# A planned one-core kernel: later products, a half-height low part of Q, fewer row transfers, one more score buffer

## The chip, the cores and the metric

The kernel runs on one core of a Trainium2 chip. The metric is the device time of one execution in microseconds (us). The core has TensorE (PE in the profile, its weight loads PEld), VectorE (DVE), ScalarE (ACT), GpSimd (POOL) and the sync engine SP, which here issues every DMA. Each engine works through its own instructions in order.

## What is computed

One layer of a streaming encoder, for a prompt of 2048 frames and for 32 new frames with a cache, with 1024 features. Two branches read the same normalised input `h`: attention over a band of nine chunks of 64 frames, and a gated delta rule. They are gated, merged and projected, and a layer norm ends the layer.

```python
qa, ka, va, za, qkv_b, zb, a_b, b_b, gate_a, gate_b = split_projection(x @ w_in)
oa = chunk_band_attention(qa, ka, va, rel_bias)          # 8 heads of 64
ya = (oa.reshape(bsz, t, A_WIDTH) * jax.nn.silu(za)) @ w_branch_a
...
yb = (ob * jax.nn.silu(zb)) @ w_branch_b
mix = jax.nn.sigmoid(gate_a) * ya + jax.nn.sigmoid(gate_b) * yb
y = layer_norm(ALPHA * x + mix @ w_out, ln_g, ln_b)
```

Outputs are `y` for both inputs, the newest 512 rows of K and V (`nk_p`, `nv_p`), the 32 new rows (`nk_s`, `nv_s`), and the states of the other branch.

## The kernel before

**Stages.** The prompt is worked in two halves of 1024 frames. Each half has the delta rule (`phase_b`) and then attention (`phase_a`). Both run beside the projections `x @ w_in`, which are cut into jobs of 128 output columns: the matmuls `pj<-hi,whi`, `pj<-hi,wlo` and `pj<-lo,whi`, since values are split into a high and a low fp16 part. The projections are PE's bulk work, and whatever else PE has to do lies between them. At the end `merge` multiplies the branches by their output weights (`a<-ghi,whi` and others) and finishes the rows.

**What sets the order.** The program is written out when it is built. Generators (one for each job, score, product and so on) run in a small event planner, the class `Flow` (line 163 on), that keeps a clock for every engine and for the DMA queue. An instruction is laid down when its generator's turn comes by these clocks, and so each engine's order is fixed. `Engine.price` gives the planned time of an instruction, and `Flow.transfer` that of a DMA. A DMA transpose is issued by `turn`. The planner gives it SP's usual 0.5 us for the issue, then its size over a rate, and then `MARGIN` = 1.6 us. What `turn` returns is the planned landing, and the product is laid down no earlier than that. On the chip only semaphores count: an instruction laid too early waits, and all that is behind it on its engine waits with it. The profile gives almost every instruction one line, L269, since `Engine` makes them all; `dma` is L292 and `turn` is L303. So the tile names tell the operations apart.

**Attention** (`phase_a`). Heads are worked in four pairs. A pair has jobs for V, K, Q and the gate z:

- `job_v`: V into `vf`, then split and turned by DMA into `vt`. In the second half V's newest 512 rows go out through `rows_out`.
- `job_k`: K split into `kst`, 128 rows for each head: high part in the head's own 64 rows, low part in the other 64.
- `job_q`: Q split into a high part `qd`, which stands in both row halves, and a low part `ql`. In `ql` each head has 128 rows, of which the 64 that aren't its own are zeros, written once for each of two buffers. Each block of Q needs four transfers for `qd` and two for `ql`, one for each head.

For each of the 8 tiles of 128 frames, and each of the 2 heads, there is a `score` and a `product`. `score` multiplies `qd` and `ql` with `kst` in one or two pieces of at most 512 keys into a PSUM bank (`a<-kst,qd`, `a<-kst,ql`). VectorE adds the bias and takes the maximum, into a score buffer `sb`. ScalarE makes the exponential, a split into two fp16 parts goes into `pu`, and `turn` lays them out transposed in `pt`. `product` multiplies `pt` with `vt` (`c<-vt,pt`, 3 matmuls for each 128 keys), then frees the buffer `pt`. Once both heads are through, `store` scales the result, turns it on PE (`b<-ident,ob`), multiplies it by the gate `ga`, which comes by DMA from `za`, and writes `g`.

Buffers: 3 each of `sb`, `pu` and `pt` in the second half, 4 in the first.

**Row outputs.** `rows_out` turns 128 columns at a time on PE into a bank of their own, copies them with ScalarE into one of two buffers `ro`, and sends them out, one transfer for each 128 rows. V's 512 rows take four transfers, K's last two blocks (272 and 240 rows) three and two, and the 32 new rows one.

**The new frames** (`sample`) have scores of their own. There the 32 rows' Q (`qs`) and the cached K are read in the head's own 64 rows only: `a<-part,qs` and `a<-ks,qs`, fp32 matmuls of 64 rows by 32 columns.

Of the kernel before, what the change touches and what calls it, by code (L numbers as in the profile page):

```python
# [11 lines left out]
F32 = mybir.dt.float32  # L12
# [45 lines left out]
    ORDER += [(_p, 0), (_p, 1), (_p, 2), (_p - 1, 3)] + [None] * FILL[_p]  # L58
ORDER += [(NP - 1, 3)]
MARGIN = 1.6  # L60
LEAD = 5.0
ZERO = 1.2
BLOCKS = [
# [214 lines left out]
def trunk(ctx: ExitStack, tc: tile.TileContext, x_p, x_s, cache_k, cache_v, st_conv, st_gdn,  # L278
# [11 lines left out]
    def dma(dst, src, eng=nc.sync):  # L290

        eng.dma_start(dst, src)  # L292
        size = 2 if dst.dtype == F16 else 4
        n = size
        for k in dst.shape:
            n *= k

        n = max(n, n // (size * dst.shape[-1]) * 768)
        return flow.transfer("SP" if eng is nc.sync else "S", n)

    def turn(dst, src):

        nc.sync.dma_start_transpose(dst, src)  # L303
        n = 2 * P
        for k in dst.shape[1:]:
            n *= k
        return flow.transfer("SP", n * 1.5)

    def gate(n):
        return Gate(flow, n)  # L310
# [21 lines left out]
    def pt(tag):  # L332

        return bank_pool[tag].tile([P, 512], F32, tag=tag, bufs=banks[tag], name=tag)
# [1157 lines left out]
    def phase_a(half):  # L1492
# [5 lines left out]
        KW = base + HALF  # L1498
        done = mark()
        vf_slot, vt_slots, kst_slots, q_slots = gate(1), gate(2), gate(2), gate(2)  # L1500
        ro_slots, bias_slots, vs_slot, sample_slot = gate(2), [gate(2), gate(1)], gate(2), gate(1)
        last_block = len(BLOCKS[half]) - 1
        NPART = 4
        parts = [ap.tile([P, 2, 512], F16, name=f"part{i}") for i in range(NPART)]
# [15 lines left out]

        low_q = []
        for i in range(2):
            t = ap.tile([P, 2, HALF], F16, name=f"ql{i}")
            for h in range(2):
                G.memset(t[HS[1 - h], h], 0.0)
            low_q.append(t)
        pairs = []
        for p in range(NP):  # L1530
            k = Pair()
# [21 lines left out]

        def rows_out(src, n, dst, p):

            for t in range(0, n, P):
                m = min(P, n - t)
                yield bank["b"]
                ps = pt("b")
                PE.transpose(ps[:m, 0:P], src[:, t:t + m], ident[:])  # L1560
                yield ro_slots
                ro = ap.tile([P, P], F32, tag="ro", bufs=2, name="ro")
                S.copy(out=ro[:m], in_=ps[:m, 0:P])
                bank["b"].give()
                yield
                yield dma(dst[t:t + m, p * P:(p + 1) * P], ro[:m])
                ro_slots.give()

        def job_v(k):
            p = k.p  # L1570
# [8 lines left out]
            def rest():  # L1579
# [32 lines left out]
                if last:  # L1612
                    yield bank["b"]
                    ps = pt("b")
                    PE.transpose(ps[:DEC, 0:P], vf[:, KW:KW + DEC], ident[:])
                    k.v_s = ap.tile([DEC, P], F32, tag="v_s", bufs=2, name="v_s")
                    S.copy(out=k.v_s[:], in_=ps[:DEC, 0:P])
                    bank["b"].give()
                    k.v_s_done.done()
                    yield  # L1620
                    yield from rows_out(vf[:, KW - BAND:KW], BAND, nv_p, p)
                    yield from rows_out(vf[:, KW:KW + DEC], DEC, nv_s, p)
                vf_slot.give()

            def evac(bi, c0, n, gcol, ps):
# [59 lines left out]
        def job_q(k):  # L1685
# [3 lines left out]
            def begin():  # L1689
                nonlocal qd, ql  # L1690

                u = k.unit = ap.tile([P, 4], F32, tag="unit", bufs=2, name=f"unit{p}")
                V.tensor_tensor(out=u[:, 0:1], in0=w_inv[:, p:p + 1], in1=w_inv[:, 4 + p:5 + p], op=ALU.mult)
                V.tensor_scalar(out=u[:, 0:1], in0=u[:, 0:1], scalar1=HD ** -0.5 / SMALL ** 2, scalar2=None, op0=ALU.mult)
                V.tensor_scalar(out=u[:, 1:2], in0=u[:, 0:1], scalar1=-1.0, scalar2=None, op0=ALU.mult)
                V.reciprocal(out=u[:, 2:3], in_=u[:, 0:1])
                V.tensor_tensor(out=u[:, 3:4], in0=w_inv[:, p:p + 1], in1=u[:, 2:3], op=ALU.mult)
                V.tensor_scalar(out=u[:, 3:4], in0=u[:, 3:4], scalar1=HD ** -0.5, scalar2=None, op0=ALU.mult)
                k.unit_known.done()
                k.qd = qd = ap.tile([P, 2, HALF], F16, tag="qd", bufs=2, name=f"qd{p}")  # L1700
                k.ql = ql = low_q[p % 2]
                k.q_s = ap.tile([P, DEC], F32, tag="q_s", bufs=2, name=f"qs{p}") if last else None

            def evac(bi, c0, n, gcol, ps):
# [13 lines left out]
                for h in range(2):  # L1718
                    for o in range(2):
                        dma(qd[HS[o], h, cs], hi[HS[h], 0:m])  # L1720
                    t = dma(ql[HS[h], h, cs], lo[HS[h], 0:m])
                yield t
                part_slots.back(place)
                if bi == last_block:
# [38 lines left out]
            pass  # L1763

        og_slots = places(4)
        NSB, NPU, NPT = (3, 3, 3) if last else (4, 4, 4)
        sbs = [ap.tile([P, KEYS], F32, name=f"sb{i}") for i in range(NSB)]
        pus = [ap.tile([P, 2 * KEYS], F16, name=f"pu{i}") for i in range(NPU)]
        pts = [ap.tile([P, 10, P], F16, name=f"pt{i}") for i in range(NPT)]
# [34 lines left out]
        def score(h, k, t, w, place, before, turn_):  # L1804
# [8 lines left out]
            for i, (s0, sn) in enumerate(pieces):  # L1813
# [2 lines left out]
                PE.matmul(ps[:, 0:sn], qd[:, h, t * P:(t + 1) * P], kst[:, h, kc + s0:kc + s0 + sn],  # L1816
                          start=True, stop=False)
                yield
                PE.matmul(ps[:, 0:sn], ql[:, h, t * P:(t + 1) * P], kst[:, h, kc + s0:kc + s0 + sn],
                          start=False, stop=True)  # L1820
                yield
                V.tensor_tensor_reduce(out=sb[:, s0:s0 + sn], in0=ps[:, 0:sn],
# [69 lines left out]
        def store(k, t, gt, w):  # L1892
# [4 lines left out]
            for z, (c0, n, _) in zip(k.z, BLOCKS[half]):  # L1897
                if c0 < (t + 1) * P:
                    yield z
            at = dma(ga[:], za_dram[k.p][:, gt * P:(gt + 1) * P])  # L1900
            yield
            ob = obs[place]
            for h in range(2):
# [520 lines left out]
```

## Time and profile before

| | us |
|---|---|
| median of 3 runs (2076.62 to 2083.29) | 2080.12 |
| the profiled execution, its own time | 2078.09 |
| its span in the profile | 2076.3 |
| PE busy | 1930.5 |
| DVE busy | 1400.7 |
| ACT busy | 972.5 |
| POOL busy | 796.0 |
| first half's attention, roughly | 550 to 800 |
| second half's attention, roughly | 1350 to 1700 |

How to read it: the profile shows one execution. "Busy" is the time in which an engine had an instruction of the program in work. A matmul row such as `c<-vt,pt 128*128 128x64 f16` names the output and inputs, the rows and columns of the weights (128 by 128), and the size and type of the moving operand. Matmuls overlap, so a row's duration (0.38 us for 512 columns) is longer than the spacing from one start to the next (0.22 us), and it is the spacing that adds up. In brackets stands how long the engine idled before the instruction, and what ended it. `SPq` rows are DMA issues: their time is SP's, not the transfer's. PEclk and the figure behind the busy times of a stretch are the clock that TensorE was granted, as a share of the full one.

### The profile page before, as it was taken

The page shows a single profiled execution, that of the slowest core. Times are in us where ns is not written, and L with a number is a line of the kernel's source. Part 1 is how long each engine was busy: PE and PEld are TensorE (multiplying, and loading weights), DVE is VectorE, ACT ScalarE, POOL GpSimd, SP SyncE. Part 2 cuts the span into 40 slices and gives each one's busy share as a digit, 9 for nine tenths or more (in the row PEclk, how much of TensorE's full clock was granted, in tenths as well). Part 3 has the DMA queues.
Part 4 walks back from the last instruction along what each step waited for, and adds up shares of the span by engine and source line. Part 5 has one row for each costly group of instructions (what it writes and reads, how often), then busy time and mean ns, then how long its engine had stood idle before and what let it go on. Part 6 is the DMA issues. An engine that isn't in the chain of part 4 may idle for free. (4 is left out here: it accounts for less than half of the span.)

```text
span 2076.3 us, 41078 instructions
## 1 busy us (share of the span) xinstructions
PE 1930.5 (93%) x14517; PEld 1353.4 (65%) x14517; DVE 1400.7 (67%) x4498; ACT 972.5 (47%) x2002; POOL 796.0 (38%) x1139
## 2 busy tenths in 40 slices
PE   8999999999989899999999999998888879999997
PEld 5455666665444446576776777665555568999996
DVE  7789889852556658589889884254545468665665
ACT  6655545444655667665445434354646552111110
POOL 6444334333334334443333423132323245543452
PEclk9999999999999999999999999999999989999999
DMA  4124332332587775223232333466776785433331
GB/s 138 65 87 112 87 85 75 102 90 98 140 201 158 163 171 135 69 81 87 74 84 67 94 98 90 117 142 146 158 167 148 186 217 193 132 102 122 103 124 46
DMA packets 380055, 246.85 MB, mean 119 GB/s; under 512 B 251202, under 2 KB 328366, under 8 KB 379848
## 3 DMA queue, kind: packets, MB, share of 16 engines
q1 hardware_dynamic: 379848, 244.22, 44.4%
q8 instruction: 114, 1.87, 0.4%
q14 instruction: 93, 0.76, 0.1%
HBM read 140.11 MB, written 54.72 MB: 94 GB/s over the span
## 5 line engine op out<-in xcount | busy, mean ns | idle before, releaser
L269 PE MATMUL pj<-hi,whi 128*128 128x512 f16 (+2 forms) x1992 | 651.3, 342 | 10.6 <-DVE zb L269 3.1
L269 PE MATMUL pj<-hi,wlo 128*128 128x512 f16 (+2 forms) x1952 | 643.6, 342 | 0.6 <-POOL wlo L269 0.5
L269 PEld LDWEIGHTS <-whi 128*128 128x128 f16 x3984 | 414.7, 106 | 226.0 <-issue 11.9
L269 PE MATMUL pj<-lo,whi 128*128 128x512 f16 (+2 forms) x1992 | 460.3, 343 | 0.0
L269 POOL TENSOR_TENSOR wlo<-wraw,whi 128x256 f16<-128x256 f32 x384 | 266.7, 718 | 497.4 <-ACT whi L269 369.5
L269 PEld LDWEIGHTS <-wlo 128*128 128x128 f16 x1952 | 207.1, 106 | 122.8 <-issue 16.6
L269 ACT CAST mh<-sg 128x256 fp32r<-128x256 f32 x64 | 25.8, 407 | 278.2 <-DVE sg L269 259.1
L269 ACT ACTIVATE wraw<-wraw,w_scale 128x1024 f32<-128x1024 f32 (+1 forms) x98 | 111.4, 1136 | 84.2 <-DVE w_scale L269 82.7
L269 ACT ACTIVATE sb<-sb,mx,unit 128x640 f32<-128x640 f32 (+4 forms) x128 | 108.5, 848 | 68.9 <-DVE mx L269 59.1
L269 PE MATMUL a<-ghi,whi 128*128 128x256 f32 (+1 forms) x512 | 134.4, 292 | 6.7 <-DVE sg L269 6.1
L269 POOL TENSOR_TENSOR pu<-sb,pu 128x640 f16<-128x640 f32 (+2 forms) x64 | 81.7, 1277 | 146.1 <-ACT pu L269 92.9
L269 ACT CAST whi<-wraw 128x512 f16<-128x512 f32 (+1 forms) x196 | 119.2, 611 | 33.3 <-PE pj L269 30.5
L269 PE MATMUL c<-vt,pt 128*128 128x64 f16 x1680 | 74.6, 198 | 64.5 <-DMA pt<-pu 61.4
L269 PE MATMUL a<-ghi,wlo 128*128 128x256 f32 (+1 forms) x512 | 132.0, 288 | 1.1 <-POOL wlo L269 1.0
L269 PEld LDWEIGHTS <-pt 128*128 128x128 f16 x1680 | 65.8, 101 | 98.8 <-DMA pt<-pu 87.1
L269 DVE TENSOR_TENSOR sys_u<-sys_u,sys_t 128x60 f32<-128x60 f32 (+24 forms) x527 | 124.6, 242 | 5.7
L269 DVE CUSTOM_DVE_ANT_0 sb<-a,bias 128x320 f32<-128x320 f32 (+5 forms) x136 | 66.5, 498 | 77.0 <-PE a L269 71.5
L269 DVE SCALAR_TENSOR_TENSOR acc<-raw,cwT,acc 128x512 f32<-128x512 f32 x144 | 112.8, 783 | 8.1 <-ACT acc L269 6.8
L269 DVE TENSOR_TENSOR sys_t<-sys_u,sys_p 128x60 f32<-128x60 f32 (+21 forms) x459 | 110.0, 243 | 5.5
L269 PEld LDWEIGHTS a<-ghi,whi 128*128 128x128 f32 x512 | 99.5, 194 | 8.3 <-DVE sg L269 6.7
L269 PEld LDWEIGHTS a<-ghi,wlo 128*128 128x128 f32 x512 | 98.9, 193 | 1.9 <-POOL wlo L269 1.2
L269 POOL TENSOR_TENSOR w_scale<-w_scale,mhalf 128x1 f32<-128x1 f32 x49 | 31.7, 648 | 168.1 <-DVE w_scale L269 120.0
(345 smaller groups left out, 4013.5 us busy)
## 6 DMA issues: line engine op xcount, KB each, us to landing
wraw<-in_w_in SPq DMA_DIRECT2D x192, 256.0 KB
sg<-sig SPq DMA_DIRECT2D x112, 128.0 KB
sig<-sig SPq DMA_DIRECT2D x44, 256.0 KB
sys_p<-sol_p SPq DMA_DIRECT2D x68, 128.0 KB
x<-in_x_p SPq DMA_DIRECT2D x16, 512.0 KB
xt<-in_x_p SPq DMA_DIRECT2D x16, 512.0 KB
out_y_p<-xt SPq DMA_DIRECT2D x16, 512.0 KB
glo<-g SPq DMA_DIRECT2D x14, 512.0 KB
```

Of the source, the lines that this page charges most:

```text
L269: r = f(*a, **k)
```

## The change

- `turn`: the planner's SP clock goes on by 0.8 us more for each transpose, and the planned landing by `SLACK` = 2.5 us. The planned landing of the gate `ga` in `store` goes back by the same. These change only the order that is laid down.
- `ql` has one 128-row tile for both heads, without zeros, in two buffers. A block's transfer is one instead of two. The score's second matmul reads the head's own 64 rows of `ql` and of `kst`, where K's high part stands.
- `rows_out` turns up to 512 columns into one bank, copies whole tiles at once into one buffer `ro` of 512 columns, and sends the full tiles in one transfer and the rest in another. V's 32 new rows are sent from the copy that `sample` reads, without another turn on PE.
- The second half's score buffers `sb` are 4 instead of 3.

```diff
+SLACK = 2.5
...
     def turn(dst, src):
...
-        return flow.transfer("SP", n * 1.5)
+        flow.busy["SP"] = max(flow.busy.get("SP", 0.0), flow.cur.clock + 0.2) + 0.8
+        return flow.transfer("SP", n * 1.5) + SLACK
...
-        ro_slots, bias_slots, vs_slot, sample_slot = gate(2), [gate(2), gate(1)], gate(2), gate(1)
+        ro_slots, bias_slots, vs_slot, sample_slot = gate(1), [gate(2), gate(1)], gate(2), gate(1)
...
-        low_q = []
-        for i in range(2):
-            t = ap.tile([P, 2, HALF], F16, name=f"ql{i}")
-            for h in range(2):
-                G.memset(t[HS[1 - h], h], 0.0)
-            low_q.append(t)
...
         def rows_out(src, n, dst, p):
 
+            full = n // P
+            yield bank["b"]
+            ps = pt("b")
             for t in range(0, n, P):
                 m = min(P, n - t)
-                yield bank["b"]
-                ps = pt("b")
-                PE.transpose(ps[:m, 0:P], src[:, t:t + m], ident[:])
-                yield ro_slots
-                ro = ap.tile([P, P], F32, tag="ro", bufs=2, name="ro")
-                S.copy(out=ro[:m], in_=ps[:m, 0:P])
-                bank["b"].give()
-                yield
-                yield dma(dst[t:t + m, p * P:(p + 1) * P], ro[:m])
-                ro_slots.give()
+                PE.transpose(ps[:m, t:t + P], src[:, t:t + m], ident[:])
+            yield ro_slots
+            ro = ap.tile([P, 512], F32, tag="ro", bufs=1, name="ro")
+            if full:
+                S.copy(out=ro[:, 0:full * P], in_=ps[:, 0:full * P])
+            m = n - full * P
+            if m:
+                S.copy(out=ro[:m, full * P:(full + 1) * P], in_=ps[:m, full * P:(full + 1) * P])
+            bank["b"].give()
+            yield
+            cs = slice(p * P, (p + 1) * P)
+            at = 0.0
+            if full:
+                at = dma(dst[0:full * P, cs].rearrange("(t q) d -> q t d", q=P),
+                         ro[:, 0:full * P].rearrange("q (t d) -> q t d", d=P))
+            if m:
+                at = dma(dst[full * P:n, cs], ro[:m, full * P:(full + 1) * P])
+            yield at
+            ro_slots.give()
...
-                    yield from rows_out(vf[:, KW:KW + DEC], DEC, nv_s, p)
+                    yield dma(nv_s[:, p * P:(p + 1) * P], k.v_s[:])
...
-                k.ql = ql = low_q[p % 2]
+                k.ql = ql = ap.tile([P, HALF], F16, tag="ql", bufs=2, name=f"ql{p}")
...
                     for o in range(2):
                         dma(qd[HS[o], h, cs], hi[HS[h], 0:m])
-                    t = dma(ql[HS[h], h, cs], lo[HS[h], 0:m])
+                t = dma(ql[:, cs], lo[:, 0:m])
...
-        NSB, NPU, NPT = (3, 3, 3) if last else (4, 4, 4)
+        NSB, NPU, NPT = (4, 3, 3) if last else (4, 4, 4)
...
-                PE.matmul(ps[:, 0:sn], ql[:, h, t * P:(t + 1) * P], kst[:, h, kc + s0:kc + s0 + sn],
+                PE.matmul(ps[:, 0:sn], ql[HS[h], t * P:(t + 1) * P], kst[HS[h], h, kc + s0:kc + s0 + sn],
                           start=False, stop=True)
...
-            at = dma(ga[:], za_dram[k.p][:, gt * P:(gt + 1) * P])
+            at = dma(ga[:], za_dram[k.p][:, gt * P:(gt + 1) * P]) + SLACK
```

## The prediction

> **What bounds the kernel now.** I read the page first, then busy time by stretch, then who TensorE (PE) waited for, then the timelines of SP and PE around the longest waits. The page's sums and slices:
>
> ```profile
> PE 1930.5 (93%) x14517; PEld 1353.4 (65%) x14517; DVE 1400.7 (67%) x4498; ACT 972.5 (47%) x2002; POOL 796.0 (38%) x1139
> PE   8999999999989899999999999998888879999997
> PEclk9999999999999999999999999999999989999999
> ```
>
> PE is busy 93% of the span, far ahead of the others, so a microsecond of PE work or of PE idling anywhere counts whole. The dips lie where attention runs: slices 11 to 14 (first half) and 27 to 32 (second half), the only stages that the change touches. Busy time in those two stretches (columns: stretch; length, PE, PEld, DVE, ACT, POOL busy; granted clock, DMA share, GB/s):
>
> ```profile
> 550.00:850.00 300.00, 265.91 (x2058) 153.96 (x2057) 189.16 (x653) 187.62 (x374) 114.59 (x146) 0.97 0.68 160
> 1350.00:1700.00 350.00, 297.62 (x2634) 198.15 (x2632) 184.76 (x653) 194.13 (x407) 99.03 (x101) 0.93 0.70 160
> ```
>
> PE idles 34.1 us in the first and 52.4 us in the second, 86.5 of the 145.8 us (2076.3 - 1930.5) that it idles in all. Who ended that idling, over the whole span:
>
> ```profile
> PE c L269 <- DMA pt<-pu: 61.4, 42, 3.8
> PE b L269 <- DVE ga L269: 7.9, 7, 2.3
> ```
>
> The first row is the products `c<-vt,pt`: 42 of the 128 blocks of them stood in PE's queue before the transposed probabilities `pt` had landed. One such wait, on SP (which issues all DMAs in order) and on PE:
>
> ```profile
> 1519.81 0.59 SPq L292 DMA_DIRECT2D ql<-part  x1
> 1520.51 0.52 SPq L292 DMA_DIRECT2D bias<-ext_dram  x1
> 1521.13 1.11 SPq L292 DMA_DIRECT2D qd<-part  x2
> 1522.33 0.55 SPq L292 DMA_DIRECT2D ql<-part  x1
> 1522.93 1.24 SPq L292 DMA_DIRECT2D qd<-part  x2
> 1524.21 0.60 SPq L292 DMA_DIRECT2D ql<-part  x1
> 1524.92 1.34 SPq L303 DMA_TRANSPOSE pt<-pu  x1
> ```
>
> ```profile
> 1523.89 0.63 PE L269 MATMUL pj<-lo,whi 128*128 128x272 f16 x4
> 1528.34 0.61 PE L269 MATMUL c<-vt,pt 128*128 128x64 f16 x15 [3.83 <-DMA pt<-pu]
> ```
>
> SP issues without a break for 5 us, the transpose comes last, and the product starts 3.42 us after that issue began (1528.34 - 1524.92). PE's order had put it 3.83 us too early. The program's planner gave a transpose 0.5 us of SP's time; the trace says 1.34.
>
> Such a stop also costs clock. The stretch before the stop, the stop, and what follows:
>
> ```profile
> 1520.00:1524.40 4.40, 4.40 (x31) 2.84 (x29) 0.67 (x2) 0.69 (x1) 0.00 (x0) 1.00 0.53 137
> 1524.40:1528.40 4.00, 0.17 (x3) 0.06 (x3) 0.94 (x4) 0.00 (x0) 0.00 (x0) 1.00 0.58 124
> 1528.40:1536.50 8.10, 8.10 (x74) 5.75 (x75) 3.60 (x16) 2.86 (x6) 0.73 (x2) 0.79 0.55 132
> ```
>
> The granted clock falls from 1.00 to 0.79 for the 8.1 us after it: about 1.7 us more (0.21 x 8.1).
>
> **The change, part by part.** The sum is made against the profiled execution's own 2078.09 us (span 2076.3 and 1.8 around it), 0.1% under the median 2080.12.
>
> *Products later.* Planned landing moves back by 2.5 us, and the planner's SP clock by 0.8 us for each transpose. PE's order at the start of the first half's attention, before (`pt` names the transposed tile, `qd` and `ql` Q's high and low part, `pj` the projection that fills the gaps):
>
> ```order
> L269 LDWEIGHTS pt_5997
> L269 MATMUL c<-vt_6085,pt_5997 128x64
> L269 LDWEIGHTS whi
> L269 MATMUL pj<-hi_162,whi 128x512
> L269 LDWEIGHTS wlo
> L269 MATMUL pj<-hi_162,wlo 128x512
> L269 LDWEIGHTS qd_6264
> L269 MATMUL a<-kst_6168,qd_6264 128x320
> ```
>
> The same product in PE's order of the changed kernel:
>
> ```order
> L270 LDWEIGHTS qd_6258
> L270 MATMUL a<-kst_6162,qd_6258 128x320
> L270 LDWEIGHTS wlo
> L270 MATMUL pj<-hi_162,wlo 128x512
> L270 LDWEIGHTS pt_5991
> L270 MATMUL c<-vt_6079,pt_5991 128x64
> L270 LDWEIGHTS ql_6259
> L270 MATMUL a<-kst_6162,ql_6259 128x320
> ```
>
> The product stood ahead of the first 320-column score; now it stands behind the second. I counted PE work between each score's last matmul and its product through both orders, at the trace's spacing of back-to-back matmuls (0.12 us for 272 columns, below, and in proportion). The mean grows from 15.1 to 18.9 us in the first half and from 12.6 to 19.6 in the second, against a longest wait of 3.8. Work fills it: the order holds the same projections. If each wait shrinks by what its own product gained, about 19 of the 64.5 us before the products stay. They stay where the distance did not grow, as at the end of the last pair:
>
> ```profile
> 1691.85 0.60 PE L269 MATMUL c<-vt,pt 128*128 128x64 f16 x15 [1.91 <-DVE ob L269]
> 1694.37 0.82 PE L269 MATMUL c<-vt,pt 128*128 128x64 f16 x12 [1.78 <-DMA pt<-pu]
> ```
>
> SP is also relieved (below), so I take 15 us left of 61.4: **-46** (5 left: -56; 35 left, if transposes come later by as much: -26).
>
> *Clock.* Of the lost clock in the two stretches ((1 - 0.97) x 300 + (1 - 0.93) x 350 = 33 us of full clock), I put about five stops like the one above, at 1.7 us, to waits that go: **-8** (0 to -17).
>
> *Q's low part without zeros.* `ql` was a 128-row operand with 64 zero rows; now its matmul reads 64 rows. Rows of before for `ql` as read and written:
>
> ```profile
> L269 PE MATMUL a<-kst,ql x224: 217/299/490, 544.5 to 1686.4; 128*128 128x320 f16 x96, 128*128 128x384 f16 x7, 128*128 128x512 f16 x5, 128*128 128x128 f16 x4
> L292 SPq DMA_DIRECT2D ql<-part x40: 525/594/1521, 535.8 to 1621.6; - x40
> L269 POOL MEMSET ql<- x8: 945/947/993, 496.7 to 1291.5; 64x1024 f16 x8
> ```
>
> Before never reads a half-height fp16 operand with 128 columns, but it has 64-row matmuls among 128-row ones: the new frames' scores (`64*32` is 64 rows by 32 columns):
>
> ```profile
> 1375.36 0.28 PE L269 MATMUL pj<-hi,whi 128*128 128x272 f16 x1
> 1375.57 0.61 PE L269 MATMUL a<-part,qs 64*32 64x512 f32 x1
> 1376.03 0.59 PE L269 MATMUL a<-part,qs 64*32 64x512 f32 x1
> 1376.55 0.29 PE L269 MATMUL pj<-hi,wlo 128*128 128x272 f16 x1
> 1376.67 0.28 PE L269 MATMUL pj<-hi,whi 128*128 128x272 f16 x1
> 1376.79 0.28 PE L269 MATMUL pj<-hi,wlo 128*128 128x272 f16 x1
> 1377.14 0.63 PE L269 MATMUL pj<-lo,whi 128*128 128x272 f16 x4
> 1377.69 0.24 PE L269 MATMUL a<-ks,qs 64*32 64x32 f32 x2
> 1377.87 0.41 PE L269 MATMUL pj<-lo,whi 128*128 128x272 f16 x2
> ```
>
> Between 128-row matmuls of 272 columns the spacing is 0.12 us (1376.67 to 1376.79). Into 64 rows it is 0.21 (1375.36 to 1375.57): 0.09 more. Within 64 rows it is 0.46 (1375.57 to 1376.03), and out of them 0.52 (1376.03 to 1376.55): 0.06 more, and the next spacing may take another 0.01. So a visit to the 64-row form costs about 0.17 us, with the array draining twice. In the changed order the 224 `ql` matmuls stand in 208 separate runs, 198 of them alone (the last row of the fence above shows one between a product and a projection). 208 x 0.17 = **+36** on PE, nothing to hide it. Bounds: 0.14 and 0.21 give +29 and +44; nothing at all is a rival. The Trainium skill, "TensorEngine Tiling (Array Packing)", Key Properties, says that changing the tiling mode drains TensorE, while changing the tile within a mode does not. It gives no price; by that rule alone this part is a loss, and the spacings above agree.
>
> *Fewer transfers on SP.* 20 of the 40 `ql` issues go (20 x 0.59 = 12 us). So do 12 of 16 for the V rows and 4 of 20 for the K rows:
>
> ```profile
> L292 SPq DMA_DIRECT2D out_nk_p<-ro x20: 355/416/812, 1342.7 to 1638.9; - x20
> L292 SPq DMA_DIRECT2D out_nv_p<-ro x16: 338/382/655, 1340.8 to 1650.3; - x16
> ```
>
> That is 12 x 0.38 + 4 x 0.42 = 6 us more. SP's order around the transpose of the quoted wait, before (its row is the last):
>
> ```order
> L292 DMA qd_18632<-part_16103 64x512 x2
> L292 DMA ql_16105<-part_16103 64x512
> L292 DMA bias_18728<-ext_dram_99 128x640
> L292 DMA qd_18632<-part_16102 64x272 x2
> L292 DMA ql_16105<-part_16102 64x272
> L303 DMA_TRANSPOSE pt_16117<-pu_16114 128x10x128
> ```
>
> And in the changed kernel, up to the transpose of the same product:
>
> ```order
> L293 DMA ql_18538<-part_16091 128x272
> L304 DMA_TRANSPOSE pt_16104<-pu_16101 128x10x128
> L293 DMA qd_18537<-part_16092 64x240 x4
> L293 DMA ql_18538<-part_16092 128x240
> L293 DMA out_nv_s<-v_s 32x128
> L293 DMA bias_18718<-ext_dram_100 128x640
> L293 DMA ga_16107<-za_89 128x128
> L293 DMA out_nk_p<-ro 128x2x128
> L293 DMA out_nk_p<-ro 16x128
> L304 DMA_TRANSPOSE pt_16102<-pu_16099 128x10x128
> ```
>
> Each block of Q brings one `ql` transfer instead of two, and K's rows of a block go out in two. The 18 us are off the path by themselves: they are part of why 15 and not 19 us of waits stay.
>
> *The rest.* The planner's 2.5 us on `ga` put its multiplication later on VectorE; half of the 7.9 us of `PE b <- DVE ga` may go: **-4** (0 to -8). Larger row copies, eight memsets fewer on POOL, four small transposes fewer on PE, and a fourth score buffer have slack: ACT and POOL are under 63% and 39% busy in both stretches. If the longer copy of V's rows were on the path, it would cost 0.58 instead of a first piece's 0.26 us in each of four pairs, 1.3 us:
>
> ```profile
> L269 ACT COPY ro<-b 128x128 f32<-128x128 f32 (+3 forms) x39 | 9.8, 259 | 47.0 <-PE b L269 22.9 <-DMA out_nk_p<-ro 15.9 <-PE a L269 5.3
> L269 ACT COPY part<-b 128x512 f32<-128x512 f32 x4 | 2.3, 580 | 1.0 <-PE b L269 1.0
> ```
>
> The single row buffer makes the next rows wait for a landing, on ScalarE; behind it stand exponentials, whose late end reaches PE only through `pt`, in the term above.
>
> Sum: -46 - 8 + 36 - 4 = -22, so 2078.1 becomes 2056, and on the median's scale **2058 us**. Its own range, with the ends of the terms taken together in part: 2035 to 2077.
>
> **The rivals.**
>
> 1. *The waits come back, slower.* SP issues in order and was solid for 5 us ahead of the quoted transpose. If transposes are late because SP and the chain before it cannot go faster, PE merely reaches each product as far ahead again. With 45 us of waits left, no clock won back, and the 36 us of switches, it is 2078 - 16 + 36 = 2098, 2100 on the median's scale. Even is at 26 us left without any other gain, at 38 with the clock and `ga` terms. Against it: the order gives 7 us more distance in the second half where waits were at most 3.8, and SP has fewer rows. For it: places like this one, where the order now holds the product 5.8 us nearer its score and the wait was already 3.33:
>
> ```profile
> 645.55 0.66 PE L269 MATMUL c<-vt,pt 128*128 128x64 f16 x9 [3.33 <-DMA pt<-pu]
> ```
>
> 2. *Half-height matmuls cost nothing.* The extra spacing may belong to fp32 operands or to 32 columns, and an fp16 operand of 64 rows by 128 columns might pass like any other: -46 - 8 - 4 = -58, 2020, or 2022 on the median's scale. The spacings speak against it, but with other types and widths. The Trainium skill, "TensorE: Matmul & The Clock Gate" (Why this matters for your kernels), says that a small-K matmul takes the time of a full one, which would be this case; the measured spacing around it decides.
>
> 3. *They cancel.* 30 us or so of waits left and 40 of switches: -31 - 4 + 40 is +5 at most, and around zero with a little clock: 2074 to 2086.
>
> **How the numbers follow.** The forecast has 0.60, rival 1 0.17, rival 2 0.09, rival 3 0.14. Faster by over 0.3% (6.2 us, about what a measurement of this kernel can tell from no change) takes the forecast and rival 2, with an edge of the forecast on the other side: 0.68. Within 0.3%: 0.15; slower: 0.17. The range 2032 to 2090 reaches past the forecast's own range on both sides and leaves out rival 2 and the worse part of rival 1.
>
> **What would show it right or wrong.** Right: `PE c <- DMA pt<-pu` at 5 to 35 us; `a<-kst,ql` shown as `64*128`, with about 0.09 us more into it and 0.06 out of it; a granted clock over 0.95 in the second stretch. Wrong if that wait stays above 40 us (rival 1), if spacings around `ql` do not grow (rival 2), or if a new row of over 15 us stands among PE's waits, such as scores waiting for VectorE.

## The result and the profile after

The changed kernel takes 2074.04 us (median of 19 runs, 2070.44 to 2078.22), the one before 2079.59 us in the same session (median of 19, 2076.41 to 2085.61). The ratio is 0.9974 [0.9965, 0.9982]: 5.5 us faster, inside the 0.3% that the forecast took for no change, and to which it gave a chance of 0.15. The forecast was 2058 us, 22 us faster. The time is in the range, and three quarters of the gain are missing.

The profiled execution of the changed kernel took 2077.25 us (span 2075.5). The page's sums, and the clock by slices:

```profile
PE 1962.4 (95%) x14513; PEld 1340.9 (65%) x14513; DVE 1409.3 (68%) x4498; ACT 969.8 (47%) x1982; POOL 786.6 (38%) x1131
PEclk9999999999998999999999999999989979999999
```

PE works 31.9 us longer than before (1962.4 against 1930.5) and idles 32.7 us less (2075.5 - 1962.4 = 113.1 against 145.8). The two nearly cancel. Busy time in the two stretches of attention:

```profile
550.00:850.00 300.00, 282.24 (x2072) 149.80 (x2072) 196.21 (x656) 190.53 (x375) 114.46 (x147) 0.97 0.67 160
1350.00:1700.00 350.00, 314.70 (x2621) 191.44 (x2620) 186.07 (x651) 190.89 (x386) 97.07 (x99) 0.92 0.72 161
```

The whole growth of PE's busy time lies here (16.3 and 17.1 us). The granted clock did not rise: 0.97 and 0.92, against 0.97 and 0.93. Who ended PE's idle time, the longest rows of the list over the whole span:

```profile
PE c L270 <- DVE ob L270: 15.4, 11, 2.9
PE pj L270 <- ACT kr L270: 7.3, 4, 2.5
PE c L270 <- DMA pt<-pu: 6.1, 6, 3.1
PE a L270 <- DVE sg L270: 5.8, 3, 3.8
PE pj L270 <- ACT vf L270: 5.0, 2, 3.3
```

The products' wait for their transposed probabilities fell from 61.4 to 6.1 us, by more than forecast (15 left). But a product now waits for `ob`: VectorE has not yet scaled the last result out of the `c` bank. This was 2.8 us before. Projections wait more too. Both are seen in the groups:

```profile
L270 PE MATMUL pj<-hi,whi 128*128 128x512 f16 (+2 forms) x1992 | 650.5, 342 | 25.5 <-ACT kr L270 7.3 <-ACT vf L270 5.0 <-DVE mx L270 5.0
L270 PE MATMUL c<-vt,pt 128*128 128x64 f16 x1680 | 73.7, 198 | 23.5 <-DVE ob L270 15.4 <-DMA pt<-pu 6.1 <-DMA ga<-za 1.9
```

The group of products idles 23.5 us instead of 64.5, the group of projections 25.5 instead of 10.6. So 41 us went in the one and 15 came back in the other. One of the new waits, on PE, near the end of the second half:

```profile
1667.60 0.30 PE L270 MATMUL a<-kst,qd 128*128 128x320 f16 x1
1667.83 0.31 PE L270 MATMUL a<-kst,ql 64*128 64x320 f16 x1
1668.07 0.31 PE L270 MATMUL a<-kst,qd 128*128 128x320 f16 x1
1671.23 0.81 PE L270 MATMUL c<-vt,pt 128*128 128x64 f16 x15 [2.86 <-DVE ob L270]
```

And VectorE at that time:

```profile
1669.24 0.82 DVE L270 TENSOR_TENSOR pu<-sb,pu 128x640 f16<-128x640 f32 x1 [1.75 <-ACT pu L270]
1669.98 0.35 DVE L270 SCALAR_TENSOR_TENSOR ga<-b,gsc,ga 128x128 f32<-128x128 f32 x1
1670.24 0.16 DVE L270 RECIPROCAL rs<-rs 128x2 f32<-128x2 f32 x1
1670.32 0.47 DVE L270 CUSTOM_DVE_ANT_0 sb<-a,bias 128x320 f32<-128x320 f32 x1
...
1670.71 0.47 DVE L270 TENSOR_SCALAR ob<-c,rs 128x64 f32<-128x64 f32 x2
```

VectorE works through these in order. It sits behind the low part of the probabilities (`pu`), which itself waited 1.75 us for ScalarE, then does a gate, a reciprocal and a score, and only at 1670.71 reads `c`. The product starts 0.5 us later. A wait for a transfer has become a wait for VectorE, which had waited for ScalarE.

The PE rows above also show the price of a half-height matmul. From the start of `qd` to that of the 64-row `ql` are 0.23 us, from `ql` to the next matmul 0.24. The same at full height, in the kernel before:

```profile
1675.54 0.30 PE L269 MATMUL a<-kst,qd 128*128 128x320 f16 x1
1675.67 0.30 PE L269 MATMUL a<-kst,ql 128*128 128x320 f16 x1
1675.81 0.27 PE L269 MATMUL b<-ident,ob 128*128 128x128 f32 x1
```

They are 0.13 and 0.14. Over both whole traces, for 320 columns at full clock and without idling, the median is 0.136 us either way before, and 0.232 into and 0.239 out of the 64-row form after. So a visit costs about 0.10 us in and 0.10 out, 0.20 where the forecast had 0.17, and 208 visits some 42 us where it had 36. The loads of `ql`'s weights at these places, in the changed kernel and in the kernel before, differ too:

```profile
1667.83 0.09 PEld L270 LDWEIGHTS <-ql 64*128 64x128 f16 x1 [0.16 <-issue]
```

```profile
1675.54 0.10 PEld L269 LDWEIGHTS <-ql 128*128 128x128 f16 x1
```

At full height the load starts together with the `qd` matmul ahead of it (1675.54). At half height it starts 0.23 us after that matmul (1667.60), and runs beside its end only. Over all 224 loads the median is 0.00 us after the start of the matmul ahead before, and 0.31 us in the changed kernel. That this later load makes the longer spacing fits in size, but was not tested.

The Trainium skill's rule on drains ("TensorEngine Tiling (Array Packing)", Key Properties) agrees. The Trainium skill's line that a small-K matmul takes the time of a full one ("TensorE: Matmul & The Clock Gate", Why this matters for your kernels) holds for the matmul's own row (0.31 against 0.30 us), but not for the spacing around one that stands alone among full-height ones.

### The profile page after: what moved, and what is told of

Same layout as the page of the kernel before. It is cut to its first block, busy times and chain, and to the rows that moved or that the text cites. A ratio compares the mean times of both kernels' runs of the same rounds, so it can differ in the third digit from the quotient of the medians.

```text
span 2075.5 us, 40953 instructions
## 1 busy us (share of the span) xinstructions
PE 1962.4 (95%) x14513; PEld 1340.9 (65%) x14513; DVE 1409.3 (68%) x4498; ACT 969.8 (47%) x1982; POOL 786.6 (38%) x1131
## 4 chain that ended last, share of the span: by engine, by line
PE 63%; DVE 15%; issue 6%; DMA 5%; ACT 5%; POOL 4%; SPq 2%; POOLq 0%; DVEq 0%; ACTq 0%
PE pj L270 36%; PE a L270 11%; PE b L270 9%; PE x L270 3%; PE c L270 2%; DVE acc L270 2%; DVE sys_t L270 2%; DVE sys_u L270 2%; POOL wlo L270 2%; PE o L270 2%; SPq L293 1%; DVE kd_bd L270 1%; DMA pt<-pu 1%; DMA sg<-sig 1%; ACT wraw L270 1%
## 5 line engine op out<-in xcount | busy, mean ns | idle before, releaser
L270 PE MATMUL pj<-hi,whi 128*128 128x512 f16 (+2 forms) x1992 | 650.5, 342 | 25.5 <-ACT kr L270 7.3
L270 PEld LDWEIGHTS <-whi 128*128 128x128 f16 x3984 | 407.3, 105 | 242.8 <-issue 14.4
L270 POOL TENSOR_TENSOR w_scale<-w_scale,mhalf 128x1 f32<-128x1 f32 x49 | 31.9, 652 | 175.5 <-DVE w_scale L270 104.4
L270 PE MATMUL c<-vt,pt 128*128 128x64 f16 x1680 | 73.7, 198 | 23.5 <-DVE ob L270 15.4
```

Source lines behind the costliest of these rows:

```text
L270: r = f(*a, **k)
```

## The experiments

Two theories stood at the start. *PE alone*: PE is the only pace, the terms were right in kind, and one of them was mis-sized. *Second pace*: in the attention stages SP's issuing in order, and the engines that wait behind it, set a pace of their own, close behind PE's; work added to PE is then partly free, and waits taken from PE come back under other names. A third joined after the first runs: that the order of instructions, which a planner lays anew for every edit, moves the time by itself. Below, "us" beside a ratio is the ratio's distance from 1 times 2078.

### The parts one by one

**Later alone**: the kernel before, with the planner's three numbers only.

```diff
+SLACK = 2.5
...
-        return flow.transfer("SP", n * 1.5)
+        flow.busy["SP"] = max(flow.busy.get("SP", 0.0), flow.cur.clock + 0.2) + 0.8
+        return flow.transfer("SP", n * 1.5) + SLACK
...
-            at = dma(ga[:], za_dram[k.p][:, gt * P:(gt + 1) * P])
+            at = dma(ga[:], za_dram[k.p][:, gt * P:(gt + 1) * P]) + SLACK
```

> The kernel before with the planner's later products alone (2.5 us on transposes and on the gate, 0.8 us of SP's planned time); Q's low part stays 128 rows with zeros. Theory (the later products are worth what they were forecast to be worth, and the half-height matmuls eat it): the wait for pt falls under 10 us, the clock in 1350 to 1700 us rises to 0.95 or more, and the time is 2030 us, from 2020 to 2042. Rival (the removed waits only turn into waits for other things, so that the later products are worth little): 2060 to 2075 us, with PE's idle time in the two stretches over 60 us.

Measured: 2071.3 us, 0.9968 [0.9956, 0.998], 6.6 us faster, as the rival had it. PE's longest waits:

```profile
PE c L270 <- DMA pt<-pu: 21.5, 17, 3.0
PE b L270 <- ACT ro L270: 17.7, 13, 3.7
PE a L270 <- DVE sg L270: 6.0, 3, 3.8
PE c L270 <- DVE ob L270: 5.5, 3, 3.7
```

Forty microseconds of product waits went (61.4 to 21.5), yet PE's idle time fell only from 145.8 to 139.7 us (span 2071.1, busy 1931.4). The second row is new against the kernel before: matmuls wait for the bank `b`, which ScalarE holds until it has copied new cache rows to `ro`. One such wait, on PE, on ScalarE and in SP's queue:

```profile
1512.23 0.48 PE L270 MATMUL b<-ident,ob 128*128 128x128 f32 x1 [3.73 <-ACT ro L270]
```

```profile
1496.15 0.27 ACT L270 COPY ro<-b 128x128 f32<-128x128 f32 x1
...
1507.20 0.27 ACT L270 COPY ro<-b 128x128 f32<-128x128 f32 x1 [3.94 <-DMA out_nv_p<-ro]
...
1511.91 0.27 ACT L270 COPY ro<-b 128x128 f32<-128x128 f32 x1 [3.75 <-DMA out_nk_p<-ro]
```

```profile
1499.64 2.57 SPq L293 DMA_DIRECT2D kst<-part  x4
1502.31 2.24 SPq L293 DMA_DIRECT2D wraw<-in_w_in  x2
1504.64 0.38 SPq L293 DMA_DIRECT2D out_nv_p<-ro  x1
1505.12 1.11 SPq L293 DMA_DIRECT2D qd<-part  x2
...
1509.46 0.44 SPq L293 DMA_DIRECT2D ga<-za  x1
1510.00 0.38 SPq L293 DMA_DIRECT2D out_nk_p<-ro  x1
```

The rows in the two `ro` buffers were copied by 1496.4. Their stores were issued at 1504.64 and 1510.00, since SP was full with loads of K, weights and Q. The next copy on ScalarE stood 3.75 us until the second store had landed, and PE stood 3.73 us behind that copy. SP's queue stands behind this wait, as it stood behind the quoted wait of before, by another way.

**Half height alone**: the kernel before, with `ql` of one tile without zeros, one transfer a block and a 64-row matmul.

```diff
-                k.ql = ql = low_q[p % 2]
+                k.ql = ql = ap.tile([P, HALF], F16, tag="ql", bufs=2, name=f"ql{p}")
...
-                    t = dma(ql[HS[h], h, cs], lo[HS[h], 0:m])
+                t = dma(ql[:, cs], lo[:, 0:m])
...
-                PE.matmul(ps[:, 0:sn], ql[:, h, t * P:(t + 1) * P], kst[:, h, kc + s0:kc + s0 + sn],
+                PE.matmul(ps[:, 0:sn], ql[HS[h], t * P:(t + 1) * P], kst[HS[h], h, kc + s0:kc + s0 + sn],
```

> The kernel before with Q's low part in half height alone. Theory: each visit to the 64-row form costs about 0.2 us of PE as in the changed kernel, 208 visits are 42 us, of which some falls into waits for pt that are still there: 2105 to 2122 us. Rival (the switch costs nothing that shows, and the changed kernel is slow for its rows or its waits): 2075 to 2085 us.

Measured: 2091.38 us, 1.0071 [1.0054, 1.0088], 14.8 us slower, between the two expectations. Its sums and its first wait:

```profile
PE 1956.7 (94%) x14517; PEld 1335.0 (64%) x14517; DVE 1402.7 (67%) x4498; ACT 972.2 (47%) x2002; POOL 789.1 (38%) x1131
```

```profile
PE c L269 <- DMA pt<-pu: 43.2, 35, 4.2
```

PE is busy 26.2 us longer, and its product waits are 18.2 us shorter without any change of the planner's numbers. Time added between a score and its product is time for the transpose to land. The edit also takes 20 of the 40 `ql` issues off SP (about 12 us), so the 14.8 us are the price of both together.

**Later and half height together** (both edits above, rows and score buffers as before):

```diff
+SLACK = 2.5
...
-                k.ql = ql = low_q[p % 2]
+                k.ql = ql = ap.tile([P, HALF], F16, tag="ql", bufs=2, name=f"ql{p}")
```

> Later products and half height together, with the old row copies and three score buffers in the second half. Theory (these two make up the result): 2074 us, give or take 6. Rival (the row copies with one buffer, or the fourth score buffer, hold the changed kernel back or push it on by more than 6 us): outside 2066 to 2082 us.

Measured: 2087.22 us, 1.005 [1.0034, 1.0067], 10.4 us slower. The two parts add up nearly (-6.6 + 14.8 = 8.2). So what is missing to the whole change, new rows and a fourth score buffer, is worth 15.8 us here (0.9974 against 1.005), where the forecast had put them at zero. In the two profiles the wait for row copies falls (`PE b <- ACT ro`, from 12.7 to 2.7 us), but PE's idle time does not (111.1 and 113.1 us).

**Half height and rows** (with the change's `rows_out`, three score buffers, the planner as before):

```diff
-                k.ql = ql = low_q[p % 2]
+                k.ql = ql = ap.tile([P, HALF], F16, tag="ql", bufs=2, name=f"ql{p}")
...
-                yield dma(dst[t:t + m, p * P:(p + 1) * P], ro[:m])
+                at = dma(dst[0:full * P, cs].rearrange("(t q) d -> q t d", q=P),
+                         ro[:, 0:full * P].rearrange("q (t d) -> q t d", d=P))
```

> Half height and the larger row copies, with products as early as before. Theory (row copies are off the path): within 5 us of the kernel with half height alone. Rival (one row buffer stalls ScalarE, or 16 fewer transfers let SP bring pt earlier): more than 8 us away from it, in either direction.

Measured: 2082.67 us, 1.0025 [1.0013, 1.0038]: 9.6 us under half height alone, and so more than the 8 us that the rival named. The product waits fall from 43.2 to 31.7 us.

**Later and rows, full height.** Beside the full-height `ql`, the rows go out 256 columns at a time, so that their buffer fits, and the score buffers stay three:

```diff
+            for t0 in range(0, n, 2 * P):
+                w = min(2 * P, n - t0)
+                full = w // P
...
+                ro = ap.tile([P, 2 * P], F32, tag="ro", bufs=1, name="ro")
```

> The kernel before with later products and larger row copies (256 columns at a time, so that it fits), without half height and with three score buffers. With later products alone PE waited 17.7 us for row copies, which the larger copies should end. Theory (the attention stages are not bound by PE alone, so only part of a removed wait is won): 2058 to 2066 us. Rival (PE is the bound, the row waits were the only reason why later products alone won so little): 2035 to 2052 us.

Measured: 2081.56 us, 1.0017 [1.0006, 1.0028], 10 us *over* later alone and above both expectations. `PE b <- ACT ro` is 22.6 us here, against 17.7 there. So the same part gained 9.6 us in one place and lost 10 in another, in part perhaps because its single buffer was halved.

### Is SP's queue a second pace?

**A gate's load in two halves**: the kernel before, with 64 more issues on SP and not a byte more.

```diff
-            at = dma(ga[:], za_dram[k.p][:, gt * P:(gt + 1) * P])
+            dma(ga[0:HD], za_dram[k.p][0:HD, gt * P:(gt + 1) * P])
+            at = dma(ga[HD:P], za_dram[k.p][HD:P, gt * P:(gt + 1) * P])
```

> The kernel before with each of the 64 loads of the gate split into two halves of 64 rows: 32 issues more on SP in each attention stage, about 0.45 us each, the same bytes. Theory (SP's in-order issue, 80 to 90% taken in these stages, sets their pace beside PE): 15 to 29 us slower than before. Rival (SP has room, the pace is set by PE and the engines): within 5 us of before.

Measured: 2117.23 us, 1.0191 [1.0174, 1.0208], 39.7 us slower. The issues of this load, in the kernel before and here (durations in ns: least, median, most):

```profile
L292 SPq DMA_DIRECT2D ga<-za x64: 319/496/2510, 562.6 to 1694.6; - x64
```

```profile
L292 SPq DMA_DIRECT2D ga<-za x128: 444/591/1777, 562.0 to 1730.5; - x128
```

By the medians SP has 128 x 0.591 - 64 x 0.496 = 43.9 us more to issue (40.4 when the rows of this load are summed one by one), and the time grows by 39.7: nearly all of it, and more than the 15 to 29 us expected. PE has the same 14517 matmuls. It idles 24.8 us more and is busy 13.0 us longer, at a lower mean granted clock (0.966 against 0.973). This is what the second pace says and PE alone does not. In the kernel before, SP's issues fill 84% of the time from 555 to 795 us and 80% from 1375 to 1695 us.

**K and Q copies issued by ScalarE**: the kernel before, with 160 transfers moved off SP's queue.

```diff
-                    dma(kst[HS[h], h, cs], hi[HS[h], 0:m])
-                    t = dma(kst[HS[1 - h], h, cs], lo[HS[h], 0:m])
+                    dma(kst[HS[h], h, cs], hi[HS[h], 0:m], nc.scalar)
+                    t = dma(kst[HS[1 - h], h, cs], lo[HS[h], 0:m], nc.scalar)
...
-                        dma(qd[HS[o], h, cs], hi[HS[h], 0:m])
+                        dma(qd[HS[o], h, cs], hi[HS[h], 0:m], nc.scalar)
```

> The kernel before with the high parts of Q and of K issued by ScalarE, and nothing else. Theory (SP's issue sets the pace of the attention stages in the kernel before): 2045 to 2060 us, with PE's wait for pt well under 61 us. Rival (relief of SP helps only where products are laid later): 2070 to 2080 us.

Measured: 2052.43 us, 0.988 [0.9845, 0.9915], 25 us faster: more than the whole change, without a single wait laid out later. Its product waits, and the issues moved:

```profile
PE c L269 <- DMA pt<-pu: 35.1, 33, 2.6
PE b L269 <- ACT ro L269: 12.2, 7, 4.3
```

```profile
L292 ACTq DMA_DIRECT2D qd<-part x80: 468/607/1245, 532.5 to 1588.1; - x80
L292 ACTq DMA_DIRECT2D kst<-part x80: 468/488/955, 523.8 to 1562.0; - x80
```

About 94 us of issuing left SP (160 at a median of 0.587 us in the kernel before; all of SP's rows together sum to 84 us less), and a quarter of that came off the time. The rest met some other limit. The Trainium skill, "DMA: Bandwidth & Descriptors" (Issuing engines are not separate DMA queues), says that several issuing engines save only the time to initiate a transfer, usually small beside the transfer itself. Here the move won 1.2% of the run. Whether that is the time to issue alone is not shown, since the moved transfers also have a queue of their own now (packets, MB, share of the 16 DMA engines):

```profile
q1 hardware_dynamic: 367048, 235.82, 43.9%
q10 hardware_dynamic: 12800, 8.40, 1.8%
```

The split load above changed the number of issues on SP without another queue.

**The same on top of later and rows**:

```diff
-                        dma(qd[HS[o], h, cs], hi[HS[h], 0:m])
+                        dma(qd[HS[o], h, cs], hi[HS[h], 0:m], nc.scalar)
```

> The kernel with later products and larger rows at full height, and the 160 transfers of the high parts of Q and of K issued by ScalarE instead of SP: some 47 us of issue less on SP in each attention stage, as much more on ScalarE. Theory (SP's issue sets the pace): 20 us or more under the same kernel without this. Rival (SP isn't the pace, and ScalarE now is later): the same or slower by up to 20 us.

Measured: 2057.86 us, 0.9905 [0.9889, 0.9921], 23 us under the same kernel with all issues on SP (1.0017).

**K and Q on ScalarE, and half height**: if the low price of half height came from SP's pace alone, it should rise toward PE's full 42 us once SP is relieved.

```diff
-                        dma(qd[HS[o], h, cs], hi[HS[h], 0:m])
+                        dma(qd[HS[o], h, cs], hi[HS[h], 0:m], nc.scalar)
...
-                k.ql = ql = low_q[p % 2]
+                k.ql = ql = ap.tile([P, HALF], F16, tag="ql", bufs=2, name=f"ql{p}")
```

> The same, with Q's low part in half height as well. Theory (half height alone cost 15 us and not 42, because PE had been waiting for SP anyway): with SP relieved more of the 42 us shows, 25 us or more over the kernel without half height. Rival (the price is 15 us whoever sets the pace): 10 to 18 us over it.

Measured: 2066.81 us, 0.9937 [0.9916, 0.9957]: 14.4 us over the kernel without half height, as much as with SP full. The wait `PE c <- DMA pt<-pu` falls again, from 35.1 to 16.0. So SP's pace does not explain the low price. The waits explain it: PE is busy 48.7 us longer (1917.6 to 1966.3) and idles 29.2 us less, 19.1 of them in this row. PE's new work fills a wait.

### The low parts side by side

**The changed kernel, low parts adjacent**: the two pieces of a score take two banks at once, so that their `ql` matmuls stand next to each other. 208 visits to the 64-row form become 121.

```diff
+            if two:
+                yield bank["a"]
+                p1 = pt("a")
+                two_banks.give()
+            low(p0, *pieces[0], False)
+            if two:
+                low(p1, *pieces[1], True)
```

> The changed kernel with the two half-height matmuls of a two-piece score laid one behind the other: 121 visits to the 64-row form instead of 208. Theory (0.2 us for each visit, about half of it won since the other half comes back as waits): 87 x 0.2 = 17 us of PE less, 2062 to 2068 us. Rival (the price goes with each half-height matmul and not with the visit, or the stages hide all of it): 2071 to 2078 us.

Measured: 2061.01 us, 0.992 [0.99, 0.994], 11 us under the change. Its sums:

```profile
PE 1941.0 (94%) x14513; PEld 1334.8 (65%) x14513; DVE 1400.3 (68%) x4498; ACT 971.0 (47%) x1982; POOL 785.9 (38%) x1131
```

PE works 21 us less than in the change (1962.4). 87 visits at 0.20 us make 17. The price of a visit is borne out a second time, from the other side.

**And with K and Q on ScalarE**: both edits on the changed kernel.

```diff
-                        dma(qd[HS[o], h, cs], hi[HS[h], 0:m])
+                        dma(qd[HS[o], h, cs], hi[HS[h], 0:m], nc.scalar)
```

> The changed kernel with the half-height matmuls of a score laid together and the high parts of Q and of K issued by ScalarE. Theory (SP's issue and PE share the bound of the attention stages, so relief of both adds up): about 2061 - 24 = 2037 us, from 2028 to 2048, the fastest so far. Rival (once PE's switches are fewer SP is no longer the pace, so its relief brings little): 2052 to 2062 us.

Measured: 2047.17 us, 0.9853 [0.9812, 0.9893], 31 us faster than before. It has the lowest median of all and beats both kernels. Four pairs of kernels now differ by the move of K and Q to ScalarE alone. By the differences of their ratios it won 25 us (kernel before), 23 (later and rows), 28 (half height alone) and 14 (adjacent low parts).

### How much the order alone moves

Every edit makes the planner lay all instructions anew. To see what that alone does, one number of the planner was nudged by 0.1 us, in four kernels. No work changes, only the order.

```diff
-MARGIN = 1.6
+MARGIN = 1.7
```

Before, 1.7, and before, 1.5:

> The kernel before with the planner's margin on every transfer 1.7 instead of 1.6 us: no work, wait or buffer differs, only the order that comes out. It measures how far the time moves when the planner merely lays the same work in another order. Theory (such scatter is 5 to 10 us, so that differences of this size between the single parts of the change cannot be put down to the part): more than 4 us from before, in either direction. Rival (the order is robust): within 4 us of before.

> The kernel before with the planner's margin 1.5 instead of 1.6 us: a third order of the same work. Theory (orders of the same work scatter by about 10 us, and the order of before may have been a lucky one): between 2080 and 2100 us. Rival (the margin itself matters, and a smaller one is as good as a larger one is bad): 2060 to 2074 us.

Later alone, 1.7 and 1.5:

> Later products alone, with margin 1.7. Theory (later products are worth some 15 to 20 us on the mean over orders, and a single order hides it): 2062 to 2076 us, 14 or more under the kernel before at 1.7 (2090). Rival (later products are worth 7 us or less in any order): 2077 us or more.

> Later products alone, with margin 1.5. So far later products gained 7 us at 1.6 and 12 at 1.7 against the same margin without them. Theory (they are worth about 10 us, not 58, in any order): 2070 to 2080 us, against 2086 for the kernel before at 1.5. Rival (the gain depends on the order so much that no mean is to be had): under 2064 or over 2086 us.

The whole change, 1.7 and 1.5:

> The changed kernel with margin 1.7. Theory (the change is worth more than its one order showed): 2062 to 2079 us, 11 or more under the kernel before at 1.7 (2090). Rival (the change is worth about 5 us at every margin): 2080 to 2088 us.

> The changed kernel with margin 1.5. So far the change gained 5.5 us at 1.6 and 25 at 1.7 against the same margin without it. Theory (its mean gain is 10 to 20 us, with a scatter of about 10 from the order): 2060 to 2080 us, against 2086 for the kernel before at 1.5. Rival (the 25 us were the luck of one order): 2081 us or more.

Half height alone, 1.7:

> Half height alone, with margin 1.7. Theory (about 45 us of PE, of which the product waits that are still there take up two thirds): 10 to 20 us over the kernel before at 1.7, 2100 to 2110 us. Rival (the 15 us at 1.6 were the scatter of orders, and the price is nothing or all of it): under 2096 or over 2122 us.

Measured, as ratios to the kernel before at 1.6:

| kernel | 1.5 | 1.6 | 1.7 | mean |
|---|---|---|---|---|
| before | 1.0047 [1.0032, 1.0062] | 1 | 1.006 [1.0036, 1.0085] | 1.0036 |
| later alone | 1.0012 [0.9997, 1.0028] | 0.9968 [0.9956, 0.998] | 1.0004 [0.9988, 1.0021] | 0.9995 |
| half height alone | - | 1.0071 [1.0054, 1.0088] | 1.009 [1.0058, 1.0122] | - |
| the change | 0.9896 [0.9874, 0.9918] | 0.9974 [0.9965, 0.9982] | 0.9941 [0.9912, 0.997] | 0.9937 |

In microseconds, each against before at the same margin:

| kernel | 1.5 | 1.6 | 1.7 | mean |
|---|---|---|---|---|
| later alone | -7 | -7 | -12 | -9 |
| half height alone | - | +15 | +6 | - |
| the change | -31 | -5 | -25 | -21 |

The order alone moves the kernel before by up to 12 us and the change by up to 16. Of the three orders, the compared one (1.6) is the best for before and the worst for the change. Half height alone at 1.7 cost 6 us, less than the 10 to 20 expected. A difference of some 10 us between two kernels that were each laid once says little. That holds for the rows (9.6 gained, 10 lost), for the 11 us of the adjacent low parts in time (its 0.992 lies among the change's three), and for the 15.8 us of rows and the fourth buffer. It does not touch the 40 us of the split load, which was laid in one order, nor the moved issues, which won 14 to 28 us in four pairs.

The waits themselves repeat in each order (us; "before" and "later alone" at 1.5, 1.6, 1.7):

| | before | later alone |
|---|---|---|
| `PE c <- DMA pt<-pu` | 72.3, 61.4, 61.9 | 12.2, 21.5, 20.6 |
| `PE b <- ACT ro` | 4.5, none, 9.8 | 17.4, 17.7, 18.0 |
| PE's idle time in all | 155.7, 145.8, 165.4 | 142.7, 139.7, 149.3 |
| PE's busy time in all | 1923.6, 1930.5, 1922.8 | 1934.8, 1931.4, 1926.6 |
| PE's idle time, 1350 to 1700 us | 59.5, 52.4, 59.3 | 58.7, 55.3, 55.2 |
| granted clock, 1350 to 1700 us | 0.94, 0.93, 0.93 | 0.91, 0.89, 0.89 |
| stops of PE over 1.5 us, both attention stretches | 29, 21, 20 | 25, 20, 24 |
| half-clock periods that begin there, us in all | 54.6, 64.8, 58.0 | 99.0, 95.6, 95.6 |

The last rows, counted in the traces, say more than the first. A stop is idle time of PE before one matmul; in a half-clock period the granted clock is 0.5. In the second half's stretch PE idles about as long as before, and its stops are about as many. Mostly their names changed.

## Why the prediction was wrong

**Products later, -46.** The wait named did go: by 40 to 60 us in three orders, and to 6.1 us in the change. The step that failed is the one from this wait to the time. It took the wait's length as time won. PE's idle time fell by only 6 to 16 us; the rest came back as waits for the row copies, for `ob`, and before projections. One of the forecast's own signs of being wrong came true: a new row of over 15 us among PE's waits (`PE c <- DVE ob`, 2.8 before, 15.4 after). Rival 1 had part of the reason (SP cannot go faster) but the wrong sign to look for: it expected the row `pt<-pu` to stay above 40. The row fell, and the time stayed. Rival 3 (they cancel, 2074 to 2086 us) had the time, at its edge: its 40 us of switches came, its 30 us of product waits left did not.

**Clock, -8.** It was not won back. The forecast drew its rule from one stop, and in the kernel before the rule holds for others: after 7 of the 8 stops of over 2.5 us in the two stretches, the mean granted clock of the next 8 us is under 0.95. But the stops did not go (21 before, 20 with later products, at 1.6), and the time at half clock grew by 31 to 44 us in the three orders. At 1.6, 10 of the 12 half-clock periods of the second stretch last 3.4 us before; with later products 3 of 11 do, and the others last 6.8 or 10.2 us. Why they last longer is open. PE's busy time is 1 to 11 us longer for the same work; that the lower clock makes it so is likely, but was only argued. Both terms together were -58 (with `ga`, whose wait went too, from 7.9 to 1.5 us). Measured, the part is worth -7 to -12.

**Half height, +36.** The mechanism and nearly the size were right on PE: 0.20 us a visit, 42 in all by the spacings. In four pairs of kernels that differ by this edit alone, PE's busy time grows by 26.2 (kernel before), 39.2 (later products), 40.5 (margin 1.7) and 48.7 us (K and Q on ScalarE). But "nothing to hide it" was wrong. Alone the edit costs 15 and 6 us of time in two orders, and 14 with SP relieved, since the work stands between scores and products that PE would have waited for. Part of the small price is the 12 us of `ql` issues that the same edit takes off SP, worth some 3 to 11 us by the rates in the next paragraph; no run parts them. The two large terms lay on the same path. They could not be added as if each stood alone: what one adds, the other's wait gives back.

**Rows, SP's issues and the fourth score buffer, "off the path".** This is the second failed step. In these stages issuing on SP is on the path: 44 us more of it cost 40, and 94 us less won 25. By these two rates 18 us of issues fewer are worth an estimated 5 to 16 us, not zero. The 12 us for `ql` are in the half-height part; the 6 us for rows come to 2 to 5. How much of the 15.8 us between the two parts and the whole change is theirs, how much the fourth buffer's and how much the order's, stays open; no run has the fourth buffer alone.

**The sum.** At the compared order, -6.6 (later) + 17.0 (half height on top of it: 1.005 against 0.9968) - 15.8 (the rest) = -5.4. The forecast had -58 + 36 + 0 = -22. Not one of the three terms was near. Over three orders the change gains 21 us on the mean, by chance about the forecast's number; with spreads of 12 and 16 us in three orders each, the mean is good to some 6 us (its standard error from these six ratios). Even so the forecast's reasons did not make it: later products are worth -9 on the mean, not -58.

**The range** held the result, but for other reasons than it gave. It had no term for the order itself. An edit of which all that counts is a few numbers of a planner needs one: here about 10 us to either side.

## What to carry to other kernels

A wait of the busiest engine is worth only what the next limit allows. Before adding up wait rows, double one suspected cost of another queue (here 64 issues on SP) and see whether the time moves; if it does, relieve that queue first. Where a planner lays the order, lay each kernel several times with a number nudged, and credit no part with less than their spread. Half-height matmuls want to stand together, since each lone one cost PE 0.20 us here.

## What the chip showed that was not expected

- 64 more DMA issues on one engine, with no more bytes, cost 39.7 us of 2078, and 160 moved to another engine won 25, with the DMA engines themselves at 0.65 to 0.80 of their time in the two stretches either way.
- An fp16 matmul of 64 rows among full-height ones costs 0.10 us on the way in and 0.10 on the way out, and its weight load starts 0.31 us after the matmul ahead of it (median), no longer together with it. The price is a little more than the fp32 ones with 32 columns (0.09 and 0.06).
- With less waiting on PE in all (6 to 16 us) the granted clock of the second half's attention was lower (0.89 to 0.91 against 0.93 to 0.94), not higher. The stops of over 1.5 us were about as many, and the time at half clock grew from 55 to 65 us to 96 to 99 us in the two stretches.
